# An encoder layer's attention leaves its softmax undivided until the output projection loads it, and VectorE takes a further share of the modulation's half columns

## The chip, the cores and the metric

The kernel runs on one core of one Trainium2 chip. That core has TensorE (PE in the profile; its weight loads are PEld), VectorE (DVE), ScalarE (ACT), GpSimd (POOL) and SyncE (SP), which here issues nearly all of the DMA transfers. The metric is the device time of one execution in microseconds (us); lower is better.

## What is computed

The layer takes x (1024 positions of 1024 features) and a conditioning vector c, and returns x after a mixer and a feed-forward part, in float32. The parts that the change touches are these:

```python
cond = jax.nn.silu(c)
mod = cond @ w_ada[l] + b_ada[l]                       # w_ada is 1024 x 6144
sh1, sc1, g1, sh2, sc2, g2 = jnp.split(mod, 6, axis=-1)
h = modulate(rms_norm(x, norm_mix_g[l]), sh1, sc1)
proj = h @ w_in[l]                                     # q, k, v of attention; qk, v, o, gates of the mLSTM
q_a, k_a, v_a, qk_m, v_m, o_m, gates = jnp.split(proj, splits, axis=-1)
y_attn = axial_gqa_attention(q_a, k_a, v_a, ...)       # 8 heads of 64, 2 heads of keys and values
y_mem = bidirectional_mlstm(qk_m, v_m, o_m, gates, ...)
mix = jnp.concatenate([y_attn, y_mem], axis=-1) @ w_out[l]
x = x + g1[:, None, :] * mix
...
# in axial_gqa_attention, for each block of 128 queries:
    s = jnp.einsum('bkgqd,bksd->bkgqs', q_blk, kt).astype(jnp.float32) * scale
    p = jax.nn.softmax(s, axis=-1).astype(vt.dtype)    # exp(s - max) / sum
    return jnp.einsum('bkgqs,bksd->bkgqd', p, vt)
```

The division by the sum is a factor for each query and head. It can be put on p (1024 numbers for each query) or on the product of p with the values (64 numbers for each query and head).

## The kernel before

**Precision.** A product of the projections is made of three matmuls (`mm3`, L322 to L325): both operands are split into a high and a low part (names ending in hi/lo or h/l), and high by high, low by high and high by low are summed in PSUM. ScalarE makes the high part as a copy, VectorE or GpSimd the low part as a subtraction. Each tile that is loaded for a projection so needs ScalarE and then VectorE or GpSimd before TensorE can use it.

**Stages** (times of the profiled execution): modulation and the first projections to about 142 us, the entry to attention to 161, attention to 485, the entry to the mLSTM to about 500, the mLSTM with the output projection to about 660, then the feed-forward part and the end at 1326.

**What sets the order of the work.** One Python program writes all engines' instructions in one order, and each engine executes its own in that order. The order is found by a planner inside the kernel: `Clock` keeps an estimated time for each engine (`Engine.cost`), `ck.chain` appends steps each of which is emitted once the one before is estimated to be done, and `streams` emits TensorE's work from several generators, the mains first and the fills where no main is ready. An entry of `bg` makes a step wait in the plan until its engine is free. So a step with another estimated cost can move all instructions that come after it. Nearly every operation of VectorE, ScalarE and GpSimd is emitted in one helper and has line L102; groups are told apart by tiles. DMAs have L328, and SyncE issues them in the written order: one that must wait holds those behind it.

**Modulation.** `w_ada` is read in columns of 128. The 64 half columns from column 16 on are loaded by `ada_late`, two ahead (`bufs=ahead`). While the list `calm` is not empty (until attention begins), VectorE multiplies a half with `cond` and sums it in one instruction (9 halves, tiles `ada<-ada,cond` on DVE). Later GpSimd multiplies and ScalarE sums as it copies (55 halves: `ada<-ada,cond` on POOL and `ada<-ada` on ACT).

**Attention** goes over 64 blocks q, 8 heads of 8 blocks each. `scores` issues four matmuls of 128x512 into S (L1202), and chains: VectorE takes the maximum (`sst<-S`) and scales it, ScalarE makes P = exp(...) with the sum of each row into the small tile `sst`, VectorE takes the reciprocal of the sum, GpSimd multiplies P by it in place (`norm`, L1217, `P<-P,sst`). Only then is the flag `Pok` set, on which `turned` waits: 8 transposes of 128x128 on TensorE (T, L1234), a copy PT of the high part on ScalarE, and the low part on VectorE. `values` multiplies with the values (`av`, L1255), ScalarE and VectorE bring the result to `avt`, and a DMA writes it to the DRAM tiles `ya_d`. There are three tiles P and 8 tiles sst. The fills between are the units of the list `IN` (the rest of the input projection; "acc" for the column-wise units q and f, followed by normalisation or by the convolution's steps `xp` and `y`, and "acct" for the units t, which ScalarE copies to `vstg`).

**The entry to attention.** `att_q(0)` makes the tile `qs` of the first head: a copy on ScalarE, then a subtraction on VectorE. Ahead of it the gates of the mLSTM are prepared; the steps `soft` (ScalarE) and `logf` (VectorE, `T<-T,gt`) end with the flag `logf_ok`, and the tile `qs` lies where `gt` was. A later step, `moved`, copies T to `Fr` on ScalarE.

**The mLSTM and the output projection** run together: transposes and products of the mLSTM (`tr<-mq,mk` L2015, U L1962, with `wv` of GpSimd and `mq` loaded by SyncE), and as fills the units of `MIX`, which are rows of the output projection. `load_y` loads the projection's input: for attention (`mem` false) the tiles `yat` from `ya_d`, 4 for each half n of the positions; `yah` and `yal` are their high part (ScalarE) and low part (GpSimd). Also the last units of IN (acct) end in this stage.

Of the kernel before, what the change touches and what calls it, by code (L numbers as in the profile page):

```python
# [20 lines left out]
P = 128  # L21
# [25 lines left out]
AHEAD = 2  # L47
NP = NF // 2
IN = [("q", 2), ("q", 3), ("f", 0), ("f", 4), ("t", 2), ("f", 1),
      ("f", 5), ("f", 2), ("t", 1), ("f", 6), ("f", 3), ("f", 7), ("t", 3)]  # L50
MIX = [("o", i) for i in range(16)] + [("m", (i + 8) % 16) for i in range(16)]
FF = [("b", p) for p in range(NB)] + [("v", 0)] + [("s", (p, i)) for p in range(1, NP - 1) for i in range(2)] + [("v", NP - 1)]
SET = ["A11", "A12", "S2", "S3", "S1", "A22", "S4"]
# [207 lines left out]
def layer_kernel(ctx, tc, xT, c, w_ada, vecs, cons, rope, w_f, w_fT, w_t0, w_t, w_o, w_gu, w_d, out):  # L261
# [39 lines left out]
    mqk_d = [dram.tile([P, S], F32, name=f"mqk_d{i}") for i in range(8)]  # L301
    v_d = [dram.tile([P, NJ, 2, P], F32, name=f"v_d{i}") for i in range(2)]
    o_d = [dram.tile([P, NJ, 2, P], F32, name=f"o_d{i}") for i in range(2)]
    ya_d = [dram.tile([P, S], F32, name=f"ya_d{i}") for i in range(4)]
    x1_d = [dram.tile([P, S], F32, name=f"x1_d{i}") for i in range(KT)]
    act_d = [{m: dram.tile([P, HALF], F32, name=f"act_d{p}{m}") for m in DOWN} for p in range(NP)]
# [20 lines left out]
    def dma(dst, src, q=None):  # L327
        (q or nc.sync).dma_start(dst, src)  # L328
        on_chip = dst.space == src.space == bass.MemoryType.SB if hasattr(src, "space") else False
        return ck.dma(math.prod(dst.shape) * 4, 0.65 if on_chip else 0.5)  # L330
# [45 lines left out]
    with tc.manual_schedule():  # L376
# [777 lines left out]
        def ada_late(ahead=2):  # L1154

            n = len(adas)
            if n == 64 or n >= ahead and not (adas[n - ahead].done and adas[n - ahead].t <= ck.t):
                return
            j, i = 16 + n // 2, n % 2
            t = PP["ada"].tile([P, HALF], F32, tag="ada", name="ada", bufs=ahead)  # L1160
            if calm:
                adas.append(ck.chain(dma(t, w_ada[j][:, halves(i)]), lambda: dve.scalar_tensor_tensor(
                    t, t, 1.0, PP["cond"][:, halves(i)], op0=OP.mult, op1=OP.mult, accum_out=modacc[:, i, j:j + 1]),
                    bg=["dve"]))
                return
            adas.append(ck.chain(dma(t, w_ada[j][:, halves(i)]), lambda: gps.tensor_mul(t, t, PP["cond"][:, halves(i)]),
                                 lambda: act.activation(t, t, AF.Copy, accum_out=modacc[:, i, j:j + 1]),
                                 bg=["gps", "act"]))
# [9 lines left out]
        def att_q(h):  # L1178
            if h:
                qd = ap.tile([P, S], F32, tag="qd", name="qd", bufs=1)  # L1180
                src = q_d[h // 2][(h % 2) * DH:(h % 2 + 1) * DH]
                dma(qd[0:DH], src)
                there = ck.chain(dma(qd[DH:P], src), lambda: None)
            else:
                qd, there = q0_at
            qs = ap.tile([P, S], F32R, tag="qs", name="qs")
            Q[h] = qs, ck.chain(0.0, there, lambda: act.activation(qs, qd, AF.Copy),
                                lambda: (gps if h else dve).tensor_sub(qs[DH:P], qd[DH:P], qs[DH:P].bitcast(F32)))

        def scores():  # L1190

            for q in range(NQ):
                h, j = divmod(q, NJ)
                if j == 2 and h + 1 < AH:
                    att_q(h + 1)
                ada_late()
                g, (qs, ok) = h // 4, Q[h]
                yield [ok, k2_ok[g]] + [slot("S")] + Tem[max(q - 3, 0):max(q - 2, 0)]
                sp, f = psum_tile([P, S], "S")
                for n in range(NH):  # L1200
                    for m in range(2):
                        nc.tensor.matmul(sp[:, halves(n)], qs[:, j * P:(j + 1) * P], k2[g][m][:, halves(n)],  # L1202
                                         start=m == 0, stop=m == 1)
                ck.pe(0.87)
                st = ap.tile([P, 4], F32, tag="sst", name="sst", bufs=8)
                cq = colq[:, j, h:h + 1]

                def top(st=st, sp=sp, cq=cq):
                    dve.reduce_max(st[:, 0:1], sp, axis=AX.X)
                    dve.tensor_scalar(st[:, 1:2], st[:, 0:1], cq, -1.0, op0=OP.mult, op1=OP.mult)  # L1210

                def exp(st=st, sp=sp, cq=cq, q=q, f=f):
                    Pt[q] = ap.tile([P, S], F32, tag="P", name="P", bufs=3)
                    act.activation(Pt[q], sp, AF.Exp, bias=st[:, 1:2], scale=cq, accum_out=st[:, 2:3])
                    f.set(ck, ck.fin + LAT)

                def norm(st=st, q=q):  # L1217
                    gps.tensor_scalar(Pt[q], Pt[q], st[:, 3:4], 0.0, op0=OP.mult, op1=OP.add)

                ck.chain(LAT, top, exp, lambda st=st: dve.reciprocal(st[:, 3:4], st[:, 2:3]), norm, flag=Pok[q])  # L1220

        def turned():

# [50 lines left out]
        def load_y(mem, n):  # L1274
# [6 lines left out]
            for k in range(4):  # L1281
# [5 lines left out]

                def load(e=e, k=k):
                    t = op.tile([P, HALF], F32, tag="yat", name="yat", bufs=4)
                    arrive = dma(t, (ym_d if mem else ya_d)[k][:, halves(n)])  # L1290

                    def hi():
# [4 lines left out]
                        e[1] = op.tile([P, HALF], F32R, tag="yal", name="yal", bufs=yb)  # L1297
                        gps.tensor_sub(e[1], t, e[0].bitcast(F32))

                    ck.chain(arrive, *used, hi, lo, flag=e[2])  # L1300

                ck.chain((2.0 if mem else 0.0) + (2.5 * k if at else 0.0), *([ym_ok[k][n]] if mem else []), load)

# [1089 lines left out]
```

## Time and profile before

Three runs took 1324.91, 1325.05 and 1332.57 us; the median is 1325.05. The profiled execution took 1328.24 us, of which the span from the first to the last instruction is 1326.4, at a mean granted TensorE clock of 0.991.

| stage of the profiled execution | us | PE busy | DVE busy | ACT busy | POOL busy | granted clock |
|---|---|---|---|---|---|---|
| entry to attention, 142 to 161 | 19 | 11.02 | 18.11 | 7.24 | 6.40 | 0.82 |
| attention, 161 to 485 | 324 | 303.18 | 266.10 | 238.31 | 205.53 | 1.00 |
| in the mLSTM, 500 to 580 | 80 | 77.13 | 66.64 | 49.56 | 41.80 | 1.00 |
| whole span | 1326.4 | 1268.8 | 1044.1 | 705.8 | 524.5 | 0.991 |

In the rows of groups, "out<-in" names the tiles, then come their sizes, the count, the total busy time, the mean of one in ns, and after the second bar the engine's idle time just before, with the work that ended most of it. In rows of the timeline the first two numbers are start and length in us; a bracket at the end holds the idle time before and what ended it. In rows of waits come the total in us, how often, and the longest.

### The profile page before, as it was taken

To read this page: it belongs to the slowest core of one execution; us is meant where nothing else is said; L and a number is where in the kernel's file an instruction comes from. 1 tells how busy PE (TensorE), PEld (TensorE's weight loads), DVE (VectorE), ACT (ScalarE), POOL (GpSimd) and SP (SyncE) were. 2 spreads that over 40 slices of the span, in tenths; PEclk is the share of its full clock that TensorE was granted. 3 is DMA by queue.
4 is the path that set the end of the run, shared out by engine and by line. 5 is a ranking of instruction groups with operands and counts; after the bars stand their busy time and mean duration, and the time that the engine had idled before them with its cause. 6 is when DMAs were issued, how large, how long until landed. Compare 5 with 4: busy or idle time off the path is not lost.

```text
span 1326.4 us, 19735 instructions
## 1 busy us (share of the span) xinstructions
PE 1268.8 (96%) x6656; PEld 1071.9 (81%) x6656; DVE 1044.1 (79%) x1679; ACT 705.8 (53%) x1349; POOL 524.5 (40%) x455
## 2 busy tenths in 40 slices
PE   9999789999899999999999999999999998999997
PEld 7887678878887888787877888888888886888886
DVE  7958798879578956898789988866676755788886
ACT  6583667877587746555686332233332334454453
POOL 0072467766476515532153355544555420000002
PEclk9999899999999999999999999999999999999999
DMA  9547423333233237633552443323333259733324
GB/s 375 196 151 196 127 99 121 96 94 106 81 120 94 64 117 259 202 100 124 191 184 71 159 135 128 112 104 115 109 104 110 88 192 335 274 100 93 94 60 163
DMA packets 104469, 187.04 MB, mean 141 GB/s; under 512 B 11568, under 2 KB 33200, under 8 KB 104368
## 3 DMA queue, kind: packets, MB, share of 16 engines
q1 hardware_dynamic: 91120, 163.81, 38.1%
q10 hardware_dynamic: 13248, 21.97, 4.4%
q8 instruction: 53, 0.87, 0.3%
q14 instruction: 48, 0.39, 0.1%
HBM read 139.33 MB, written 42.73 MB: 137 GB/s over the span
## 4 chain that ended last, share of the span: by engine, by line
PE 65%; DVE 16%; ACT 6%; DMA 5%; issue 4%; POOL 4%; SPq 0%; ACTq 0%; DVEq 0%; POOLq 0%
PE acc L325 16%; PE acc L323 16%; PE acc L324 16%; DVE x L102 3%; PE av L1255 3%; PE T L1234 3%; PE S L1202 2%; DVE sst L102 2%; DVE y L102 2%; DVE PT L102 2%; DVE wlo L102 1%; PE acct L323 1%; POOL wlo L102 1%; PE acct L325 1%; PE acct L324 1%
## 5 line engine op out<-in xcount | busy, mean ns | idle before, releaser
L102 ACT ACTIVATE whi<-wst 128x512 fp32r<-128x512 f32 (+2 forms) x223 | 133.9, 607 | 140.8 <-PE acc L325 62.7
L102 POOL TENSOR_TENSOR wlo<-wst,whi 128x512 fp32r<-128x512 f32 x80 | 123.2, 1547 | 162.3 <-ACT whi L102 110.9
L324 PE MATMUL acc<-x,whi 128*128 128x512 f32 x352 | 136.9, 389 | 0.0
L102 DVE TENSOR_TENSOR wlo<-wst,whi 128x512 fp32r<-128x512 f32 (+2 forms) x143 | 94.3, 664 | 33.2 <-ACT whi L102 32.8
L102 POOL TENSOR_SCALAR P<-P,sst 128x1024 f32<-128x1024 f32 x64 | 84.3, 1319 | 77.3 <-DVE sst L102 69.0
L102 DVE TENSOR_TENSOR PT<-T,PT 128x512 fp32r<-128x512 f32 x128 | 84.8, 682 | 24.7 <-ACT PT L102 24.4
L323 PE MATMUL acc<-hh,whi 128*128 128x512 f32 x224 | 96.2, 429 | 8.4 <-ACT xp L102 8.4
L102 POOL TENSOR_TENSOR x<-x,ny 128x256 f32<-128x256 f32 (+1 forms) x8 | 8.3, 1066 | 237.3 <-PE acc L325 217.1
L102 POOL TENSOR_TENSOR wlo<-wr,whi 128x512 fp32r<-128x512 f32 x52 | 72.2, 1388 | 71.8 <-ACT whi L102 68.7
L325 PE MATMUL acc<-whi,wcl 128*128 128x512 f32 x244 | 96.6, 396 | 2.6 <-DVE wcl L102 2.6
L323 PE MATMUL acc<-whi,wch 128*128 128x512 f32 x244 | 96.2, 394 | 2.3 <-ACT wch L102 2.3
L324 PE MATMUL acc<-wlo,wch 128*128 128x512 f32 x244 | 95.9, 393 | 0.0
L324 PE MATMUL acc<-hl,whi 128*128 128x512 f32 x224 | 88.7, 396 | 0.3 <-DVE hl L102 0.3
L102 ACT ACTIVATE whi<-wr 128x512 fp32r<-128x512 f32 x56 | 35.4, 632 | 100.6 <-DVE wr L102 48.3
L102 POOL TENSOR_TENSOR ada<-ada,cond 128x512 f32<-128x512 f32 x55 | 78.6, 1435 | 25.7 <-DMA ada<-in_w_ada_dram 22.6
L325 PE MATMUL acc<-hh,wlo 128*128 128x512 f32 x224 | 88.7, 396 | 0.1
L102 ACT ACTIVATE P<-S,sst,colq 128x1024 f32<-128x1024 f32 x64 | 77.2, 1206 | 21.1 <-DVE sst L102 20.7
L102 ACT ACTIVATE PT<-T 128x512 fp32r<-128x512 f32 x128 | 73.5, 597 | 26.7 <-PE T L1234 25.4
L323 PE MATMUL acct<-whi,hh 128*128 128x256 f32 (+1 forms) x256 | 77.6, 303 | 9.5 <-ACT vstg L102 8.8
L102 DVE TENSOR_REDUCE sst<-S 128x1 f32<-128x1024 f32 x64 | 77.7, 1214 | 6.2 <-PE S L1202 5.1
L1234 PE MATMUL T<-ident,P 128*128 128x128 f32 x512 | 72.8, 274 | 6.6 <-DVE PT L102 4.0
L324 PEld LDWEIGHTS acc<-x,whi 128*128 128x128 f32 x352 | 66.1, 188 | 13.7
(483 smaller groups left out, 3836.6 us busy)
## 6 DMA issues: line engine op xcount, KB each, us to landing
wr<-in_w_gu_dram SPq DMA_DIRECT2D x66, 256.0 KB, 2.7
ada<-in_w_ada_dram SPq DMA_DIRECT2D x64, 256.0 KB, 2.9
wd<-in_w_d_dram SPq DMA_DIRECT2D x22, 512.0 KB, 6.9
wst<-in_w_gu_dram SPq DMA_DIRECT2D x42, 256.0 KB, 2.9
wst<-act_d SPq DMA_DIRECT2D x33, 256.0 KB, 3.1
ada<-in_w_ada_dram SPq DMA_DIRECT2D x16, 512.0 KB, 7.4
wst<-in_w_o_dram SPq DMA_DIRECT2D x32, 256.0 KB, 3.3
act_d<-sg ACTq DMA_DIRECT2D x29, 256.0 KB, 2.1
```

Of the source, the lines that this page charges most:

```text
L102: return fn(*args, **kw)
L323: nc.tensor.matmul(acc, w[0], x[0], start=first, stop=False)
L324: nc.tensor.matmul(acc, w[0], x[1], start=False, stop=False)
L325: nc.tensor.matmul(acc, w[1], x[0], start=False, stop=last)
L1202: nc.tensor.matmul(sp[:, halves(n)], qs[:, j * P:(j + 1) * P], k2[g][m][:, halves(n)], start=m == 0, stop=m == 1)
L1234: nc.tensor.transpose(tp[:, k], Pt[q][:, (4 * b + k) * P:(4 * b + k + 1) * P], ident)
L1255: nc.tensor.matmul(av, va[:, k, h // 4], PT[it, b][m][:, k - 4 * b], start=(k, m) == (0, 0), stop=(k, m) == (NJ - 1, 1))
```

## The change

The reciprocal of the sums and its multiplication with P go away from the 64 blocks. exp now puts its sums into `colq`, the tile whose column (the scale of this block's scores) it has just used. When the last block of a head has its P, VectorE takes the reciprocal of that head's 8 columns in one instruction, and a DMA writes the 1024 numbers to a new DRAM tile `r_d`. `load_y` reads them for attention's halves: before each `yat`, two DMAs spread the numbers of two heads over 64 partitions each of a tile `yar` (two such tiles), and GpSimd multiplies `yat` by `yar` before `yah` and `yal` are made.

Beside this, `ada_late` gives every second half column to VectorE also during attention, where the planner's estimate has VectorE free within 0.3 us: 12 halves move, so that VectorE has 21 and GpSimd and ScalarE 43. The first head's `qs` is chained behind `logf_ok`, and in `IN` the unit f 6 comes before t 1.

```diff
--- before.py
+++ after.py
@@ -47,7 +47,7 @@
 AHEAD = 2
 NP = NF // 2
 IN = [("q", 2), ("q", 3), ("f", 0), ("f", 4), ("t", 2), ("f", 1),
-      ("f", 5), ("f", 2), ("t", 1), ("f", 6), ("f", 3), ("f", 7), ("t", 3)]
+      ("f", 5), ("f", 2), ("f", 6), ("t", 1), ("f", 3), ("f", 7), ("t", 3)]
 MIX = [("o", i) for i in range(16)] + [("m", (i + 8) % 16) for i in range(16)]
 FF = [("b", p) for p in range(NB)] + [("v", 0)] + [("s", (p, i)) for p in range(1, NP - 1) for i in range(2)] + [("v", NP - 1)]
 SET = ["A11", "A12", "S2", "S3", "S1", "A22", "S4"]
@@ -301,6 +301,7 @@
     mqk_d = [dram.tile([P, S], F32, name=f"mqk_d{i}") for i in range(8)]
     v_d = [dram.tile([P, NJ, 2, P], F32, name=f"v_d{i}") for i in range(2)]
     o_d = [dram.tile([P, NJ, 2, P], F32, name=f"o_d{i}") for i in range(2)]
+    r_d = [dram.tile([1, S], F32, name=f"r_d{i}") for i in range(AH)]
     ya_d = [dram.tile([P, S], F32, name=f"ya_d{i}") for i in range(4)]
     x1_d = [dram.tile([P, S], F32, name=f"x1_d{i}") for i in range(KT)]
     act_d = [{m: dram.tile([P, HALF], F32, name=f"act_d{p}{m}") for m in DOWN} for p in range(NP)]
@@ -1158,7 +1159,7 @@
                 return
             j, i = 16 + n // 2, n % 2
             t = PP["ada"].tile([P, HALF], F32, tag="ada", name="ada", bufs=ahead)
-            if calm:
+            if calm or ck.free["dve"] <= ck.now + 0.3 and n % 2:
                 adas.append(ck.chain(dma(t, w_ada[j][:, halves(i)]), lambda: dve.scalar_tensor_tensor(
                     t, t, 1.0, PP["cond"][:, halves(i)], op0=OP.mult, op1=OP.mult, accum_out=modacc[:, i, j:j + 1]),
                     bg=["dve"]))
@@ -1184,7 +1185,7 @@
             else:
                 qd, there = q0_at
             qs = ap.tile([P, S], F32R, tag="qs", name="qs")
-            Q[h] = qs, ck.chain(0.0, there, lambda: act.activation(qs, qd, AF.Copy),
+            Q[h] = qs, ck.chain(0.0, there, *([] if h else [logf_ok]), lambda: act.activation(qs, qd, AF.Copy),
                                 lambda: (gps if h else dve).tensor_sub(qs[DH:P], qd[DH:P], qs[DH:P].bitcast(F32)))
 
         def scores():
@@ -1211,13 +1212,14 @@
 
                 def exp(st=st, sp=sp, cq=cq, q=q, f=f):
                     Pt[q] = ap.tile([P, S], F32, tag="P", name="P", bufs=3)
-                    act.activation(Pt[q], sp, AF.Exp, bias=st[:, 1:2], scale=cq, accum_out=st[:, 2:3])
+                    act.activation(Pt[q], sp, AF.Exp, bias=st[:, 1:2], scale=cq, accum_out=cq)
                     f.set(ck, ck.fin + LAT)
 
-                def norm(st=st, q=q):
-                    gps.tensor_scalar(Pt[q], Pt[q], st[:, 3:4], 0.0, op0=OP.mult, op1=OP.add)
-
-                ck.chain(LAT, top, exp, lambda st=st: dve.reciprocal(st[:, 3:4], st[:, 2:3]), norm, flag=Pok[q])
+                ck.chain(LAT, top, exp, flag=Pok[q])
+                if j == NJ - 1:
+                    rq = colq[:, :, h]
+                    ck.chain(1.0, *Pok[q - j:q + 1], lambda rq=rq: dve.reciprocal(rq, rq),
+                             lambda rq=rq, h=h: dma(r_d[h].rearrange("o (j p) -> p (o j)", p=P), rq), bg=[None] * NJ + ["dve", None])
 
         def turned():
 
@@ -1287,6 +1289,9 @@
 
                 def load(e=e, k=k):
                     t = op.tile([P, HALF], F32, tag="yat", name="yat", bufs=4)
+                    r = None if mem else op.tile([P, HALF], F32, tag="yar", name="yar", bufs=2)
+                    for i in range(0 if mem else 2):
+                        dma(r[i * DH:(i + 1) * DH], r_d[2 * k + i][:, halves(n)].partition_broadcast(DH))
                     arrive = dma(t, (ym_d if mem else ya_d)[k][:, halves(n)])
 
                     def hi():
@@ -1297,7 +1302,7 @@
                         e[1] = op.tile([P, HALF], F32R, tag="yal", name="yal", bufs=yb)
                         gps.tensor_sub(e[1], t, e[0].bitcast(F32))
 
-                    ck.chain(arrive, *used, hi, lo, flag=e[2])
+                    ck.chain(arrive, *used, *([] if mem else [lambda: gps.tensor_mul(t, t, r)]), hi, lo, flag=e[2])
 
                 ck.chain((2.0 if mem else 0.0) + (2.5 * k if at else 0.0), *([ym_ok[k][n]] if mem else []), load)
 
```

TensorE has the same instructions as before (6422 rows of the program), in another order.

**ScalarE at the entry to attention**, before. Tiles have running numbers; `xp` is the convolution's or the projection's input step, `whi` a weight's high part, `P` the first block's exp.

```order
L102 ACTIVATE xp_1411<-acc_1482 128x512 [waits PE_49]
L102 ACTIVATE qs_1584<-qd0_1337 128x1024 [waits DMAHW0_49,DVE_49,Pool_49]
L102 ACTIVATE xp_1529<-acc_1532 128x512 [waits PE_49]
L102 ACTIVATE Fr_1601<-T1_1373 64x1024
L102 ACTIVATE whi_1607<-wst_1508 128x512 [waits DMAHW7_49,PE_49]
L102 ACTIVATE ada_1585,modacc_81<-ada_1585 128x512 [waits Pool_49]
L102 ACT_TABLE_LOAD [waits DVE_49,PE_49]
L102 ACTIVATE P_1646,sst_1620<-S_1612,sst_1620,colq_190 128x1024 [waits Activation_49]
```

And after:

```order
L102 ACTIVATE xp_1419<-acc_1490 128x512 [waits PE_49]
L102 ACTIVATE Fr_1596<-T1_1381 64x1024 [waits DVE_49]
L102 ACTIVATE qs_1592<-qd0_1345 128x1024 [waits DMAHW0_49,Pool_49]
L102 ACTIVATE xp_1537<-acc_1540 128x512 [waits PE_49]
L102 ACTIVATE whi_1615<-wst_1516 128x512 [waits DMAHW7_49,PE_49]
L102 ACT_TABLE_LOAD [waits DVE_49]
L102 ACTIVATE xp_1419<-y_1558 128x1024 [waits Activation_49]
L102 ACTIVATE whi_1656<-wst_1560 128x512 [waits DMAHW1_49,PE_49]
L102 ACTIVATE xp_1537<-acc_1595 128x512 [waits PE_49,Activation_49]
L102 ACTIVATE P_1659,colq_198<-S_1629,sst_1634,colq_198 128x1024 [waits DVE_49]
```

`Fr`, the copy behind the gates, now stands ahead of `qs` and of the second `xp`, on which the next matmuls wait. The half column (`ada` with `modacc`) is no longer ahead of the first P, two steps of the convolution are.

**SyncE at the first loads of the output projection**, before. `o_d` is a store of the input projection's last units, `mq` a load for the mLSTM; DMAHW names stand for earlier transfers that a DMA waits for.

```order
L328 DMA o_d1_100<-vstg_5540 128x256 [waits Activation_49]
L328 DMA yat_5570<-ya_d0_101 128x512
L328 DMA yat_5572<-ya_d1_102 128x512
L328 DMA yat_5574<-ya_d2_103 128x512 [waits DMAHW0_49]
L328 DMA yat_5576<-ya_d3_104 128x512 [waits DMAHW1_49]
L328 DMA o_d1_100<-vstg_5568 128x256 [waits DMAHW2_49,Activation_49]
L328 DMA mq_5602<-mqk_d0_89 128x256 [waits DMAHW3_49]
```

And after, from the first `yat` on (its two `yar` stand just ahead of these rows):

```order
L329 DMA yat_5454<-ya_d0_109 128x512 [waits DMAHW0_49]
L329 DMA yar_5460<-r_d2_103 64x512 [waits DMAHW1_49]
L329 DMA yar_5460<-r_d3_104 64x512 [waits DMAHW2_49]
L329 DMA yat_5459<-ya_d1_110 128x512 [waits DMAHW3_49]
L329 DMA yar_5465<-r_d4_105 64x512 [waits DMAHW6_49,DMAHW7_49,DMAHW4_49,Pool_49]
L329 DMA yar_5465<-r_d5_106 64x512 [waits DMAHW5_49]
L329 DMA yat_5464<-ya_d2_111 128x512
L329 DMA yar_5470<-r_d6_107 64x512 [waits DMAHW2_49,DMAHW1_49,Pool_49]
L329 DMA yar_5470<-r_d7_108 64x512 [waits DMAHW0_49]
L329 DMA yat_5469<-ya_d3_112 128x512
L329 DMA o_d1_100<-vstg_5452 128x256 [waits Activation_49]
L329 DMA mq_5498<-mqk_d0_89 128x256 [waits DMAHW3_49]
```

Each `yat` now has two `yar` ahead of it. The third and fourth pair wait for GpSimd, which must have used the first and second tile, and the load of `mq` stands behind all twelve transfers and a store.

**GpSimd at the same place**, before. `wv` are the mLSTM's weighted values, four for each step, the first of which waits for TensorE.

```order
L102 TENSOR_SCALAR wv_5590<-v1_5498,cols_191 128x130 [waits DMAHW1_49,Pool_49]
L102 TENSOR_SCALAR wv_5590<-v1_5498,cols_191 128x130 x3
L102 TENSOR_SCALAR wv_5651<-v1_5498,cols_191 128x130 x4
L102 TENSOR_TENSOR yal_5664<-yat_5570,yah_5648 128x512 [waits DMAHW6_49,Activation_49]
L102 TENSOR_TENSOR yal_5679<-yat_5572,yah_5662 128x512 [waits DMAHW7_49,Activation_49]
L102 TENSOR_SCALAR wv_5682<-v1_5498,cols_191 128x130 [waits PE_49]
L102 TENSOR_SCALAR wv_5682<-v1_5498,cols_191 128x130 x3
L102 TENSOR_TENSOR yal_5694<-yat_5574,yah_5674 128x512 [waits DMAHW0_49,Activation_49]
L102 TENSOR_TENSOR yal_5706<-yat_5576,yah_5690 128x512 [waits DMAHW1_49,Activation_49]
L102 TENSOR_SCALAR wv_5709<-v1_5498,cols_191 128x130 [waits PE_49]
```

And after:

```order
L102 TENSOR_SCALAR wv_5545<-v1_5382,cols_199 128x130 x4
L102 TENSOR_TENSOR yat_5454<-yat_5454,yar_5455 128x512 [waits DMAHW7_49,DMAHW6_49,DMAHW0_49]
L102 TENSOR_SCALAR wv_5563<-v1_5382,cols_199 128x130 [waits PE_49]
L102 TENSOR_SCALAR wv_5563<-v1_5382,cols_199 128x130 x3
L102 TENSOR_TENSOR yat_5459<-yat_5459,yar_5460 128x512 [waits DMAHW3_49,DMAHW2_49,DMAHW1_49]
L102 TENSOR_TENSOR yal_5598<-yat_5454,yah_5585 128x512 [waits Activation_49]
L102 TENSOR_TENSOR yat_5464<-yat_5464,yar_5465 128x512 [waits DMAHW6_49,DMAHW5_49,DMAHW4_49]
L102 TENSOR_SCALAR wv_5590<-v1_5382,cols_199 128x130 [waits PE_49]
L102 TENSOR_SCALAR wv_5590<-v1_5382,cols_199 128x130 x3
L102 TENSOR_TENSOR yat_5469<-yat_5469,yar_5470 128x512 [waits DMAHW7_49,DMAHW1_49,DMAHW0_49]
L102 TENSOR_TENSOR yal_5637<-yat_5459,yah_5625 128x512 [waits Activation_49]
L102 TENSOR_TENSOR yal_5677<-yat_5464,yah_5664 128x512 [waits Activation_49]
```

The new multiplications of `yat` by `yar` stand in turn with `wv`: one group of `wv` is between the first and the second of them, another between the third and the fourth.

## The prediction

> **What bounds the kernel now.** I read the page's first part, then the stretches in which the change lies.
>
> ```profile
> PE 1268.8 (96%) x6656; PEld 1071.9 (81%) x6656; DVE 1044.1 (79%) x1679; ACT 705.8 (53%) x1349; POOL 524.5 (40%) x455
> ```
>
> TensorE is busy for 96% of the span and keeps its instructions, so nothing can be won but its idle time and its slow clock. The stretches' columns are start and end, length, busy time of PE, PEld, DVE, ACT and POOL, granted clock, DMA share, GB/s:
>
> ```profile
> 142.00:161.00 19.00, 11.02 (x38) 8.25 (x37) 18.11 (x22) 7.24 (x11) 6.40 (x4) 0.82 0.43 138
> 161.00:485.00 324.00, 303.18 (x2014) 269.02 (x2014) 266.10 (x420) 238.31 (x479) 205.53 (x159) 1.00 0.30 94
> ```
>
> In attention TensorE idles 20.8 of 324 us, beside 8 us at the entry, where the clock also drops. No other engine is full there. What TensorE waits for from 140 to 500 us (total, times, longest):
>
> ```profile
> PE acct L323 <- ACT vstg L102: 8.8, 9, 2.0
> PE acc L323 <- ACT xp L102: 8.4, 3, 4.8
> PE T L1234 <- DVE PT L102: 4.0, 6, 1.6
> PE S L1202 <- ACT P L102: 3.2, 1, 3.2
> PE T L1234 <- POOL P L102: 2.0, 3, 1.6
> PE av L1255 <- DVE PT L102: 1.4, 3, 0.7
> ```
>
> The last steps are copies and subtractions that free or fill a buffer. Only 2.0 us are put down to GpSimd's division directly. The change must work through what stands ahead of these steps in their engines' queues.
>
> **The attention part.** The removed and moved work, per group:
>
> ```profile
> L102 POOL TENSOR_SCALAR P<-P,sst 128x1024 f32<-128x1024 f32 x64 | 84.3, 1319 | 77.3 <-DVE sst L102 69.0 <-PE T L1234 4.0 <-ACT PT L102 3.2
> L102 POOL TENSOR_TENSOR ada<-ada,cond 128x512 f32<-128x512 f32 x55 | 78.6, 1435 | 25.7 <-DMA ada<-in_w_ada_dram 22.6 <-ACT PT L102 3.0
> ...
> L102 DVE SCALAR_TENSOR_TENSOR y<-xp,vec,y 128x1024 f32<-128x1024 f32 x32 | 48.6, 1520 | 0.3
> ...
> L102 ACT ACTIVATE ada<-ada 128x512 f32<-128x512 f32 x55 | 34.6, 631 | 19.6 <-POOL ada L102 19.6
> ...
> L102 DVE RECIPROCAL sst<-sst 128x1 f32<-128x1 f32 x64 | 10.0, 157 | 16.6 <-ACT P L102 16.2
> ```
>
> ```profile
> L102 DVE SCALAR_TENSOR_TENSOR ada<-ada,cond 128x512 f32<-128x512 f32 x9 | 8.1, 907 | 8.2 <-DMA ada<-in_w_ada_dram 8.2
> ```
>
> Engine by engine: GpSimd loses 84.3 us of division and 12 x 1.435 = 17.2 of halves, half of its 205.5. ScalarE loses 12 x 0.631 = 7.6. VectorE loses 10.0 and gains 12 x 0.907 = 10.9 and eight wider reciprocals, at least 8 x 0.157 = 1.3: 2 us more. So VectorE, the fullest engine beside TensorE, gets no relief. None of these sums is on the path; what counts is whom they hold up. Two such places:
>
> ```profile
> 421.94 2.02 POOL L102 TENSOR_SCALAR P<-P,sst 128x1024 f32<-128x1024 f32 x1 [1.89 <-DVE sst L102]
> 423.92 2.23 POOL L102 TENSOR_TENSOR ada<-ada,cond 128x512 f32<-128x512 f32 x1
> ```
>
> ```profile
> 426.19 0.63 ACT L102 ACTIVATE ada<-ada 128x512 f32<-128x512 f32 x1 [2.12 <-POOL ada L102]
> ```
>
> ```profile
> 427.45 0.50 PE L323 MATMUL acc<-hh,whi 128*128 128x512 f32 x1 [2.91 <-ACT xp L102]
> ```
>
> ```profile
> 174.21 0.39 PE L323 MATMUL acct<-whi,hh 128*128 128x256 f32 x1 [2.00 <-ACT vstg L102]
> ```
>
> At 424 GpSimd's half stands behind a division, ScalarE waits 2.12 us for it, its next step `xp` comes late, and TensorE stands 2.91 us. At 174 it is the same, with `vstg`. Without divisions GpSimd takes each half as it lands, so I take both stalls as gone: -4.9 us (bounds -4.9 and 0). The direct wait for P goes too, -2.0 (bounds -2.0 and 0). Of the waits for PT, 5.4 us, I take -1.0: T now starts some 1.5 us sooner after exp, but VectorE's queue is no shorter and its order is new (bounds -4 and +3, the one near the sum of both rows, the other near what two new rows like them would cost). The other `vstg` waits have no cause here that goes: 0 (-3 to +5).
>
> A rule that speaks against the moved halves: the Trainium skill, "SBUF — State Buffer", section "Who interferes with whom", says that a VectorE instruction with two SBUF inputs and a GpSimd instruction that reads SBUF exclude one another for their whole length. The trace agrees in kind: a step y beside which GpSimd did nothing took
>
> ```profile
> 158.90 1.28 DVE L102 SCALAR_TENSOR_TENSOR y<-xp,vec,y 128x1024 f32<-128x1024 f32 x1
> ```
>
> against a mean of 1.52 in attention. By this row VectorE gains up to 32 x 0.24 = 7.7 us of time when the divisions go; I put it at no gain on the path, and it is a reason for the first rival.
>
> **The entry to attention.** ScalarE now, contiguous to the dots:
>
> ```profile
> 146.13 1.06 ACT L102 ACTIVATE qs<-qd 128x1024 fp32r<-128x1024 f32 x1 [3.70 <-issue]
> 147.09 0.58 ACT L102 ACTIVATE xp<-acc 128x512 f32<-128x512 f32 x1
> 147.69 1.06 ACT L102 ACTIVATE Fr<-T 64x1024 f32<-64x1024 f32 x1
> ...
> 157.39 0.63 ACT L102 ACTIVATE ada<-ada 128x512 f32<-128x512 f32 x1 [3.94 <-POOL ada L102]
> ```
>
> `qs` stood until 146.13, and `xp` behind it ended TensorE's wait of 4.8 us. The chaining to `logf_ok` doesn't remove this, since the tile waited for that step anyway; and `Fr`, 1.06 long, now stands ahead of both: +1.1. Ahead of the first P stood the half column, itself 3.94 us late; it is away from there, so of the 3.2 us that S waited for P I take 2.6 as gone (two other steps stand ahead of P now). Together -1.5 (bounds -3.2 and +2).
>
> **The entry to the mLSTM.** SyncE, the landings (count, size, us) and those who wait:
>
> ```profile
> 495.04 2.20 SPq L328 DMA_DIRECT2D yat<-ya_d  x4
> 497.35 0.37 SPq L328 DMA_DIRECT2D o_d<-vstg  x1
> 498.62 0.32 SPq L328 DMA_DIRECT2D mq<-mqk_d  x1
> ```
>
> ```profile
> mq<-mqk_d SPq DMA_DIRECT2D x16, 128.0 KB, 3.1
> yat<-ya_d SPq DMA_DIRECT2D x8, 256.0 KB, 5.9
> ```
>
> ```profile
> 505.30 0.61 PE L2015 MATMUL tr<-mq,mk 128*128 128x128 f32 x4
> 505.66 0.36 PE L323 MATMUL acct<-whi,hh 128*128 128x256 f32 x1
> 505.86 0.28 PE L324 MATMUL acct<-wlo,hh 128*128 128x256 f32 x1
> 505.98 0.28 PE L325 MATMUL acct<-whi,hl 128*128 128x256 f32 x1
> ```
>
> ```profile
> 504.47 1.44 POOL L102 TENSOR_SCALAR wv<-v,cols 128x130 f32<-128x130 f32 x4
> ```
>
> ```profile
> L102 POOL TENSOR_TENSOR yal<-yat,yah 128x512 fp32r<-128x512 f32 x14 | 18.9, 1355 | 32.3 <-ACT yah L102 29.4 <-DMA yat<-ya_d 2.8
> ```
>
> `mq` was issued at 498.62 and used at 505.30, with 3.6 us to spare after its 3.1. Now SyncE issues, at 0.55 us each (2.20 for four), two `yar` and the first `yat` (issued at 496.1, landed after 5.9 at 502.0), the second three, and then stands until GpSimd has multiplied the first `yat` (1.36, priced as `yal`: 503.4). Behind that GpSimd has four `wv` (1.44: 504.8) and the second product (506.2), on which SyncE's fourth triple waits. Three issues and a store make it 508.4 for `mq`, which lands at 511.5. By the order of the instructions, TensorE has 18 more acct matmuls ahead of its use, 0.12 us apart, so it comes at 505.30 + 2.2 = 507.5: a stall of 4.0 us. The second half's four loads have the same shape later; nothing in the trace shows how near it is to its use, so it lies between 0 and another 4.0, and I take 1.0, as those loads are planned further ahead. Together +5.0 (0 to +9).
>
> The eight writes of `r_d`, 1024 numbers of 4 bytes each, have no like row; DMA is busy 0.30 of the stretch, and the last is due some 20 us after attention ends: 0, at worst a later fourth triple.
>
> **The sum.** -4.9 - 2.0 - 1.0 - 1.5 + 5.0 = -4.4 us. The profiled execution would take 1328.24 - 4.4 = 1323.8; it lies 3.2 above the median, so on the median of 1325.05 the forecast is 1320.6. The terms' distances to their ends, squared and added, give roots of 6.8 downwards and 9.8 upwards: its own range is 1314 to 1330. Chance 0.50.
>
> **The rivals.**
>
> *All queue waits go.* With GpSimd half empty and its claim on VectorE's inputs gone, PT comes early too, and `mq` is absorbed: 4.9 + 2.0 + 5.4 + 3.2, half of the remaining vstg waits (3.4), less 1.1 for `Fr` is 17.8: 1307. For it speaks the mean of 1.52 for y; against it that VectorE stays at 266 of 324 us. Chance 0.20.
>
> *Slower: SyncE stands behind GpSimd.* If `mq` behind the added transfers lands as late as `yat` (5.9), it is there at 514.3 and TensorE stands 6.8 us, and the second half costs 4 more. At 142 to 161 an idle of 4.8 us came with a clock of 0.82, worth up to 0.18 x 19 = 3.4 us, where the stall of 2.91 at 427 left it at 1.00; I add 2.4. With an attention gain of 5 that is +8: 1333. It decides once `mq` lands after about 512.5. For it speaks that every step was summed without slack; against it that TensorE still has matmuls of the output projection that a planner may put there. Chance 0.18. The Trainium skill, "TensorE: Matmul & The Clock Gate", section "What's actually happening", puts the limit at an idle window of about 3.4 us and halves the clock for as long again; the two rows agree. By it the forecast's own stall of 4.0 would also cost some 1.7 us, which is inside its range.
>
> *Nothing to see.* The new order makes as many waits for `vstg` and PT as it removes (the +5 above), and the gain and loss cancel: 1325. Chance 0.12.
>
> **Range and chances.** 1305 to 1333 takes in all centres and leaves out the far ends of the first two rivals. A measurement here can tell about 1% from no change (1311.8 to 1338.3). Faster than that: nearly all of the first rival, 0.19. Slower: a third of the second, 0.06. Within: 0.75.
>
> **What would show it.** Right: no wait of ScalarE for GpSimd's `ada` above 1 us in attention, T waiting for ScalarE's P not at all, the first `xp` wait grown to about 5.9, `tr<-mq,mk` waiting 3 to 5 us for `mq` near 508, GpSimd's busy time in attention near 105 us. Wrong: waits for PT or `vstg` beyond 20 us together, or a clock below 1.00 after 500 us.

## The result and the profile after

The changed kernel takes 1398.63 us (median of 4 runs, 1397.23 to 1401.17) where the kernel before, beside it, takes 1326.28: a ratio of 1.0533, 95% interval 1.0511 to 1.0555. The forecast was 1320.6 with a range up to 1333. It was wrong by 78 us and in the direction.

The page of the changed kernel, its first line and, by the same columns as before, three stretches: the entry, attention, and ten microseconds in attention.

```profile
PE 1286.0 (92%) x6656; PEld 1089.6 (78%) x6656; DVE 1048.4 (75%) x1647; ACT 698.2 (50%) x1325; POOL 431.8 (31%) x387
```

```profile
142.00:165.00 23.00, 13.78 (x50) 10.69 (x49) 21.08 (x27) 11.05 (x17) 6.87 (x5) 0.76 0.34 104
165.00:550.00 385.00, 318.55 (x2004) 284.30 (x2002) 264.30 (x390) 229.54 (x454) 106.50 (x83) 0.91 0.34 80
199.00:209.00 10.00, 6.02 (x43) 5.29 (x41) 3.47 (x6) 3.22 (x7) 0.00 (x0) 0.98 0.27 27
```

GpSimd's load in attention fell as forecast, from 205.5 to 106.5 us. TensorE's busy time rose by 17 us over the whole span with the same number of matmuls; the granted clock in attention is 0.91 where it was 1.00, and TensorE idles 66 us there instead of 21. In the third row TensorE stands for 4 of the 10 us, VectorE and ScalarE for more than 6, GpSimd for all of them, and the transfers move 27 GB/s at a busy share of 0.27. In attention before the change they moved 94 GB/s at 0.30.

Who waits, by the first rows of waits of the changed kernel (TensorE's alone from 167 to 560 us, then three rows of all engines from 161 to 535):

```profile
PE T L1236 <- DVE PT L102: 28.7, 6, 11.2
PE av L1257 <- ACT PT L102: 16.4, 2, 8.3
PE acct L324 <- ACT vstg L102: 9.7, 5, 7.3
PE acc L324 <- ACT xp L102: 7.0, 3, 4.9
```

```profile
POOL ada L102 <- DMA ada<-in_w_ada_dram: 117.1, 20, 14.2
...
ACT qs L102 <- DMA qd<-q_d: 29.8, 3, 12.1
...
ACT ada L102 <- POOL ada L102: 21.0, 4, 9.8
```

The waits for PT and `vstg` are over 50 us together, which is the first of the prediction's own signs of being wrong (more than 20). These are few and long waits, not many short ones: ScalarE stands six times, once after each of the first six stores, for 6.6 to 12.1 us behind a transfer that came late. The first of them from its beginning, one row each of SyncE, GpSimd, ScalarE and TensorE:

```profile
195.26 0.40 SPq L329 DMA_DIRECT2D r_d<-colq  x1
195.76 1.42 SPq L329 DMA_DIRECT2D ada<-in_w_ada_dram  x1
```

```profile
210.75 1.26 POOL L102 TENSOR_TENSOR ada<-ada,cond 128x512 f32<-128x512 f32 x1 [12.96 <-DMA ada<-in_w_ada_dram]
```

```profile
212.05 0.63 ACT L102 ACTIVATE ada<-ada 128x512 f32<-128x512 f32 x1 [9.78 <-POOL ada L102]
```

```profile
213.30 1.95 PE L1257 MATMUL av<-PT,va 128*128 128x256 f32 x5 [8.29 <-ACT PT L102]
```

SyncE issues the store of the first head's reciprocals, then a half column, which lands 14.9 us later. GpSimd so starts on it only at 210.75, ScalarE its product at 212.05, the copy PT comes behind that, and TensorE stands 8.29 us and then finds its clock at 0.50 (209 to 215 us). What the store itself takes from issue to landing, in the list of DMA issues (count, size, median us):

```profile
r_d<-colq SPq DMA_DIRECT2D x8, 4.0 KB, 13.5
```

A store of 4 KB needs 13.5 us (one of the eight landings is recorded in this trace), where 256 KB of a half column need 2.9 in the median. From 195 to 199 us 1078 of the 1344 packets on record are under 512 bytes; from 199 to 209 us it is 14 of 153. The store's 1024 pieces are so on record within 4 us of its issue, but it lands at 208.8, and the other transfers are slow until then. What passes in these ten us the packets don't tell.

Stage by stage, in us, by the starts of the first S, the first and the second block of `tr<-mq`, the last `tr<-mq`, and the down projection's first product with `wch`; the last column is an experiment below, in which only the store's pieces are larger:

| stretch | before | after | stores of 32-byte pieces |
|---|---|---|---|
| start to first S | 153.6 | 159.1 | 157.4 |
| first S to first tr | 343.7 | 403.3 | 337.1 |
| first to second block of tr | 8.0 | 15.5 | 15.5 |
| to the last tr | 98.6 | 98.0 | 98.0 |
| to the down projection | 502.0 | 504.2 | 505.3 |
| to the end | 220.4 | 217.1 | 217.4 |

Of the 71 us between the spans, 60 come in attention.

### The profile page after: what moved, and what is told of

It reads as the page before. It is cut to its first block, busy times and chain, and to the rows that moved or that the text cites. A ratio compares the mean times of both kernels' runs of the same rounds, so it can differ in the third digit from the quotient of the medians.

```text
span 1397.2 us, 19494 instructions
## 1 busy us (share of the span) xinstructions
PE 1286.0 (92%) x6656; PEld 1089.6 (78%) x6656; DVE 1048.4 (75%) x1647; ACT 698.2 (50%) x1325; POOL 431.8 (31%) x387
## 4 chain that ended last, share of the span: by engine, by line
PE 61%; DVE 16%; DMA 11%; ACT 4%; issue 4%; POOL 3%; SPq 1%; ACTq 0%; DVEq 0%; POOLq 0%
PE acc L326 16%; PE acc L324 15%; PE acc L325 15%; PE T L1236 3%; PE av L1257 3%; DVE x L102 3%; DMA ada<-in_w_ada_dram 2%; PE S L1203 2%; DMA qd<-q_d 2%; DVE PT L102 2%; DVE y L102 1%; DVE sst L102 1%; PE acct L324 1%; PE acct L326 1%; PE acct L325 1%
## 5 line engine op out<-in xcount | busy, mean ns | idle before, releaser
L1236 PE MATMUL T<-ident,P 128*128 128x128 f32 x512 | 78.3, 290 | 29.4 <-DVE PT L102 28.7
L102 POOL TENSOR_TENSOR ada<-ada,cond 128x512 f32<-128x512 f32 x43 | 62.0, 1446 | 126.5 <-DMA ada<-in_w_ada_dram 117.1
L1257 PE MATMUL av<-PT,va 128*128 128x256 f32 x512 | 76.0, 294 | 20.6 <-ACT PT L102 16.4
L1236 PEld LDWEIGHTS T<-ident,P 128*128 128x128 f32 x512 | 64.0, 149 | 37.1 <-DVE PT L102 30.7
L324 PE MATMUL acct<-whi,hh 128*128 128x256 f32 (+1 forms) x256 | 80.8, 316 | 11.8 <-ACT vstg L102 9.7
L1257 PEld LDWEIGHTS av<-PT,va 128*128 128x128 f32 x512 | 69.0, 196 | 25.9 <-ACT PT L102 17.0
```

Of the source, the lines that this page charges most:

```text
L102: return fn(*args, **kw)
L324: nc.tensor.matmul(acc, w[0], x[0], start=first, stop=False)
L1236: nc.tensor.transpose(tp[:, k], Pt[q][:, (4 * b + k) * P:(4 * b + k + 1) * P], ident)
L1257: nc.tensor.matmul(av, va[:, k, h // 4], PT[it, b][m][:, k - 4 * b], start=(k, m) == (0, 0), stop=(k, m) == (NJ - 1, 1))
```

## The experiments

Theory A: a store of 1024 single numbers holds up the transfers behind it. Theory B: the new order and the moved half columns cost the time.

**The stores alone.** Edit on the kernel before:

```diff
...
                 ck.chain(LAT, top, exp, lambda st=st: dve.reciprocal(st[:, 3:4], st[:, 2:3]), norm, flag=Pok[q])
+                if j == NJ - 1:
+                    rq = colq[:, :, h]
+                    ck.chain(1.0, *Pok[q - j:q + 1], lambda rq=rq, h=h: dma(r_d[h].rearrange("o (j p) -> p (o j)", p=P), rq))
```

> The kernel before, with nothing of the change but the eight stores to r_d, at the same places (they store the scale columns of colq, and nobody reads them; the output is that of the kernel before). Theory A, that a store of 1024 single numbers holds up the transfers queued behind it: the changed kernel lost 10 to 14 us in most heads after its stores, so 1326 plus 50 to 75, that is 1376 to 1401, with the stall of ScalarE or GpSimd on a late load of queries or halves once per head. Theory B, that the new order and the moved half columns cost the time: within 1% of 1326.

Measured: ratio 1.0199 (1.0166 to 1.0232), 28 us on the spans (1354.0 against 1326.4). Eight stores of 4 KB that nobody reads cost 2%. The landings of this kernel:

```profile
r_d<-colq SPq DMA_DIRECT2D x8, 4.0 KB, 10.4
```

Six of them are recorded, at 9.6 to 11.7 us. Theory A's mechanism is there, but with 28 us where 50 to 75 were expected.

**Larger pieces.** Edit on the changed kernel; the partition's 8 numbers are put side by side on both sides:

```diff
-                    ck.chain(1.0, *Pok[q - j:q + 1], lambda rq=rq: dve.reciprocal(rq, rq),
-                             lambda rq=rq, h=h: dma(r_d[h].rearrange("o (j p) -> p (o j)", p=P), rq), bg=[None] * NJ + ["dve", None])
+                    rc = ap.tile([P, NJ], F32, tag="rc", name="rc", bufs=2)
+                    ck.chain(1.0, *Pok[q - j:q + 1], lambda rq=rq, rc=rc: dve.reciprocal(rc, rq),
+                             lambda rc=rc, h=h: dma(r_d[h].rearrange("o (p j) -> p (o j)", p=P), rc), bg=[None] * NJ + ["dve", None])
```

> The changed kernel, with the reciprocals put into a small contiguous tile and stored as 128 runs of 8 numbers (32 bytes) instead of 1024 single numbers; the loads then read the numbers in another order, so the attention half of the output projection's input is divided by the wrong sums. All instructions otherwise in the same order. Theory A: most of the 72 us goes, 1320 to 1340. Theory B: stays at 1390 to 1400.

Measured: ratio 1.0009 (0.9991 to 1.0026), span 1330.5. All of the loss but 4 us on the span is gone, with everything else of the change in place: in the two traces every engine has the same instructions in the same order, and only the store's pieces differ. (This kernel divides by the wrong sums; that changes numbers, not work.) The store of this kernel:

```profile
r_d<-rc SPq DMA_DIRECT2D x8, 4.0 KB, 1.7
```

And who waits on late transfers in attention (all engines, 161 to 510 us):

```profile
POOL ada L102 <- DMA ada<-in_w_ada_dram: 95.0, 26, 8.9
...
ACT qs L102 <- DMA qd<-q_d: 1.9, 2, 1.3
...
ACT ada L102 <- POOL ada L102: 1.5, 2, 1.2
```

ScalarE hardly stands for queries or halves any more (1.3 us at most). Theory B falls as the main cause. GpSimd still waits 95 us for halves, but nobody waits long for it, so this is idle time that it has.

**Single numbers at other places.** Edit on the changed kernel:

```diff
-dma(r_d[h].rearrange("o (j p) -> p (o j)", p=P), rq)
+dma(r_d[h].rearrange("o (p j) -> p (o j)", p=P), rq)
```

> The changed kernel, where only the places in DRAM change: still 1024 single numbers of 4 bytes, but the 8 numbers of a partition lie side by side in r_d (read in another order by the loads, so divided by the wrong sums). Theory A by the number of pieces: as slow as the changed kernel, 1390 to 1400. Theory A by scattered addresses in DRAM: near the kernel with runs of 32 bytes. Theory B: 1390 to 1400 too; this one tells the two forms of A apart.

Measured: ratio 1.0289 (1.0207 to 1.0371), span 1359.9, landings of 7.1 to 11.6 us:

```profile
r_d<-colq SPq DMA_DIRECT2D x8, 4.0 KB, 8.3
```

Between the two forms. About half of the loss goes when a partition's numbers lie together in DRAM, and the rest stays as long as they are 1024 pieces: both count. How much each counts is rough, since the two runs of this kernel lie 15 us apart (1361.71 and 1376.76), and the trace is of the faster one.

**The stores on another queue.** Edit: the store gets `nc.scalar` as its issuing engine.

> The changed kernel with the eight stores of single numbers issued by ScalarE instead of SyncE, so that they stand in another DMA queue; TensorE's instructions are the same. If the stores only hold up what stands behind them in their own queue, nearly all of the 72 us goes: 1330 to 1345, with the numbers landing as late as before. If they occupy the DMA engines themselves, or the way to DRAM, the transfers of the other queue are held up as well: 1380 to 1400.

Measured: ratio 1.0320 (1.0290 to 1.0351), span 1367.2. It lies between both statements. All transfers from 244 to 251 us, behind the second store, which ScalarE issued at 242.84, and the store `ya_d` that SyncE issued at 244.89 (64 KB, landing after 9.2 us; 1.9 is the median of this store in the changed kernel):

```profile
DMA packets 888, 0.12 MB, mean 17 GB/s; under 512 B 805, under 2 KB 869, under 8 KB 887
```

```profile
ya_d<-avt SPq DMA_DIRECT2D x1, 64.0 KB, 9.2
```

SyncE's transfers still trickle though the store stands in another queue, so what is held is shared by the queues. Some 30 us come back; how much of that is the queue, and how much that ScalarE now issues the stores, the run doesn't tell. The Trainium skill, "DMA: Bandwidth & Descriptors", section "Issuing engines are not separate DMA queues", says that transfers run on the same 16 DMA engines whoever starts them; the 17 GB/s agree with it.

**Why 28 us become 70.** Two more kernels complete a square of division (on GpSimd as before, or left to the loads) and halves (moved or not), all with the stores of single numbers. The changed kernel with `if calm:` as before:

> The changed kernel with its stores of single numbers, but all half columns after the start of attention with GpSimd and ScalarE, as before (55 and 9). The stores alone cost 28 us in the kernel before and 68 in the changed one. If the moved halves make the difference (VectorE's queue standing for a half that lands late): 1355 to 1370. If the removed division does (GpSimd and ScalarE now reach each half at once and stand there when it lands late): 1390 to 1400.

And the kernel before with the stores and the new condition:

> The kernel before (division on GpSimd kept, its load_y kept) with the eight stores of single numbers and the rule that gives VectorE every second half column (13 move). The fourth corner beside three that are known on the time: stores with division and no halves moved +28 us over before, stores without division and no halves moved +52, stores without division and halves moved +72. If the moved halves cost the same with the division as without it (20): 1373 to 1381. If GpSimd's division is what covers a late transfer, whoever takes the halves: 1352 to 1364.

Measured: ratios of 1.0394 (1.0367 to 1.0421) and 1.0217 (1.0184 to 1.0250). Spans, less the 1326.4 of before:

| | halves not moved | halves moved |
|---|---|---|
| division on GpSimd | +28 | +31 |
| division at the loads | +52 | +71 |

With the division, the moved halves cost 3 us on the span, which the ratios don't tell from nothing (1.0199 and 1.0217, with intervals that overlap); without it, 19. The lower row has the rest of the change too: the loads of `yar`, the chained first queries and the new order of units. Rows of waits of the kernel with division and without moved halves, and then of the one without either (all engines, 161 to 510):

```profile
POOL ada L102 <- DMA ada<-in_w_ada_dram: 31.2, 14, 6.1
...
ACT ada L102 <- POOL ada L102: 19.5, 16, 2.3
...
ACT qs L102 <- DMA qd<-q_d: 12.5, 4, 8.4
```

```profile
POOL ada L102 <- DMA ada<-in_w_ada_dram: 108.6, 24, 16.7
...
ACT ada L102 <- POOL ada L102: 24.2, 8, 7.6
...
ACT qs L102 <- DMA qd<-q_d: 17.0, 3, 9.3
```

With the division in its queue, GpSimd comes to a half late anyway, and one that lands 10 us late keeps ScalarE no longer than 2.3 us. Without it ScalarE stands up to 7.6 us behind GpSimd's halves (9.8 in the changed kernel). By the plan that is because each step of a half then follows right on the landing that the planner expects; no run shows this step by itself. Waits of TensorE above 3.3 us between the first S and the last av are 2, 3, 6 and 6 in the order stores alone, with halves, without division, changed kernel; they sum to 11, 18, 41 and 48 us, and at each the granted clock falls to 0.50 for 3.4 us or more. That division was cover for late halves fits all of this, and the kernel with division and moved halves came out as that account had it; but it isn't shown by itself, because each of these kernels has its own planned order and the lower row more changes than the division. Why the moved halves cost 19 without the division stays open.

**Turned on TensorE.** The repair that computes the same as the changed kernel: a head's 128x8 reciprocals are transposed into PSUM, and the store has 8 rows of 512 bytes.

```diff
-                             lambda rq=rq, h=h: dma(r_d[h].rearrange("o (j p) -> p (o j)", p=P), rq), bg=[None] * NJ + ["dve", None])
+                    def turn(rq=rq, h=h):
+                        rp, f = psum_tile([P, 4, P], "T")
+                        nc.tensor.transpose(rp[0:NJ, 0], rq, ident)
+                        ck.add_pe(0.06)
+                        rt = ap.tile([DH, 2, P], F32, tag="avt", name="rt", bufs=3)[0:NJ, 0]
...
+                        ck.chain(0.3, take, lambda: dma(r_d[h].rearrange("o (j p) -> (o j) p", p=P), rt))
...
```

> The changed kernel, with each head's 128x8 reciprocals transposed by TensorE into PSUM and copied by ScalarE to 8 rows of 128, so that the store has 8 runs of 512 bytes. 8 more small matmuls and 8 small copies. Theory A: 1318 to 1335, the forecast of before with its other terms put to the test. Theory B: above 1385.

Measured: ratio 1.0048 (1.0025 to 1.0071), span 1330.7; the median of 1336.55 lies 4 us above the profiled execution. Without the moved halves:

> The version with the numbers transposed by TensorE (8 runs of 512 bytes), without the moved halves. The forecast's term: the moved halves bring nothing of themselves, so the same within 4 us as the version with them (1331 on the trace). Rival, the port between VectorE and GpSimd: 12 fewer VectorE instructions of 0.9 us and no gain for GpSimd, 5 to 8 us faster. Rival, ScalarE's waits for GpSimd's halves come back: 5 us slower.

Measured: 1.0059 (1.0041 to 1.0077), span 1332.3, so the moved halves are worth nothing that can be seen once the stores are cheap, as the forecast had it; neither rival shows.

**Four tiles yar.** Edit on the version turned on TensorE: `bufs=4` in place of `bufs=2`.

> The version with the numbers transposed by TensorE, with four tiles yar instead of two: the same order of transfers, but the third and fourth triple no longer wait for GpSimd, so SyncE reaches the load of mq some 4 to 8 us sooner. If that wait made TensorE's stall of 4.4 us for mq: the stall is below 1 us and the span 3 to 5 us shorter, 1326 to 1328. If the bytes of the eight added loads ahead of mq made it: the stall stays at 3 to 5 us.

Measured: 1.0016 (1.0001 to 1.0031), span 1330.9. TensorE's first matmul on `mq` of the second block, with two tiles and then with four:

```profile
507.89 0.98 PE L2032 MATMUL tr<-mq,mk 128*128 128x128 f32 x3 [4.37 <-DMA mq<-mqk_d]
```

```profile
507.03 0.68 PE L2032 MATMUL tr<-mq,mk 128*128 128x128 f32 x4 [1.70 <-DMA mq<-mqk_d]
```

The stall falls by 2.7 us, so SyncE's wait for GpSimd made most of it. It doesn't fall below 1 us, as expected; the added issues and bytes may make the remaining 1.7, which no run shows. The span doesn't follow: the entry to attention was longer by about as much in this run (first S at 157.8 against 155.8). On the ratios it is 0.3% better, with intervals that overlap.

**Three attempts at the rest.** All start from the version with four tiles. The first head's queries without the chain behind the gates:

> The version turned by TensorE with four tiles yar, with the first head's queries no longer chained behind the gates: on ScalarE qs stands ahead of Fr again and the half column's place is unchanged. The forecast's price of Fr at that place is 1.1 us; the versions with the chain show TensorE's first wait for xp at 5.8 to 7.4 us, the kernel before 4.8. If Fr's place is the cause: the wait falls to 4.5 to 5.2 and the span by 1 to 3 us, 1328 to 1330, on the time at par with before or up to 0.2% faster. If something else holds qs: the wait stays at about 6.4.

Measured: 1.0078 (1.0059 to 1.0096). `Fr` stood behind `qs` again and the wait was 6.5 us all the same. That looks as if its place cost nothing, but the step of VectorE on which `Fr` and `qs` wait (`logf`, `T<-T,gt`) came later here. Starts on VectorE and of the `xp` behind `qs`, in us:

| kernel | `T<-T,gt` | `xp` | between |
|---|---|---|---|
| before | 143.88 | 147.09 | 3.21 |
| 32-byte pieces, chained | 145.04 | 149.29 | 4.25 |
| four tiles, chained | 145.54 | 149.78 | 4.24 |
| four tiles, not chained | 146.66 | 149.88 | 3.22 |

So `Fr` ahead of `qs` costs 1.0 us, as the forecast had it, and without the chain a start 1.1 us later hides it. The trace is of the slowest of the six runs (1344.51, median 1339.60). Its span, 1342.6, was lost later, in attention (346.3 us from first S to first tr, against 336.6) and in the mLSTM, where a wait of 4.0 us for VectorE's `num` went with a clock of 0.50. The units in the old order:

> The version turned by TensorE with four tiles yar, with the two units f 6 and t 1 in the order of before; the chain stays. Nothing in the forecast gave the swap a price of its own: the same within 3 us as the version with it (span 1330.9). Rival: the swap was what kept the convolution ahead of the mLSTM's loads, and without it the entry to the mLSTM is 3 to 8 us later.

Measured: 1.0061 (1.0038 to 1.0084), span 1333.2. The spans differ by 2.3 us, but the ratios by 0.45%, 6 us, with intervals that don't meet (1.0001 to 1.0031 with the swap); and the first `tr<-mq` starts at 498.4 where it was 494.4, within the rival's 3 to 8 us. So the expectation of no difference fails: the swap, which the forecast gave no price, seems to be worth some us. That the convolution is the reason isn't shown. The loads of `yar` issued by ScalarE, without the chain:

> As the one whose first queries aren't chained, with the sixteen loads yar issued by ScalarE. SyncE has only the yat ahead of mq, so if its issues (0.55 us each) make what is left of the stall for mq (1.7 us), the stall goes and the span falls by 1.5 to 3 us. If ScalarE stands at its own issues (they wait for store and slots), the copies behind it come late: 2 to 10 us slower.

Measured: 1.0122 (1.0095 to 1.0148), span 1338.8 in the fastest of four runs: the wait for `mq` is gone, but ScalarE stands 11.0 us at its own issues and TensorE 5.4 us for the `vstg` behind them. Against the version without the chain the time is some 6 us longer, by the ratios, as expected for that case. No version was faster than the kernel before.

## Why the prediction was wrong

**The step that failed** is the eight writes of `r_d`, put at "0, at worst a later fourth triple". They cost 67 us of the 71 on the spans: between the changed kernel and the one with pieces of 32 bytes nothing else differs in the order of the instructions. Two arguments behind that 0 were bad. The DMA's busy share of 0.30 was taken as room; but at 199 to 209 us the share is 0.27 while transfers that are due come 10 us late, so a low share doesn't tell room. And only the last store was asked when it is needed, not what stands behind each in the queue: halves, queries and weights. That the operation had "no like row" should have widened the range upwards, by at least eight times some unknown hold, and didn't.

The Trainium skill, "DMA: Bandwidth & Descriptors", section "Rules for kernel authors", says that a last dimension that isn't contiguous is lowered to one descriptor for each element and should be rearranged. Such a store is this one, and that was a rival to weigh. The trace agrees with the count: more than 1024 packets under 512 bytes within 4 us of the issue. The rule gives no price; the runs do: 9.6 to 13.5 us for 1024 pieces in the changed kernel and with the stores alone, 1.7 in the median for 128.

**The other terms**, read from the kernel with 32-byte pieces. Its rows of TensorE's waits, 140 to 520 us:

```profile
PE acc L324 <- ACT xp L102: 8.8, 3, 6.7
PE tr L2021 <- DMA mq<-mqk_d: 5.7, 2, 4.6
PE T L1237 <- DVE PT L102: 5.5, 6, 2.2
PE av L1258 <- DVE PT L102: 4.0, 5, 1.6
PE acct L324 <- ACT vstg L102: 2.9, 5, 1.0
PE acct L324 <- ACT xp L102: 2.4, 2, 2.2
```

- ScalarE's waits for GpSimd's halves: forecast to go (-4.9). They fell from 19.6 us (the entry included) to 1.5. Right. TensorE's waits for `vstg` fell from 8.8 to 2.9, of which only 2.0 was forecast; the other `vstg` waits, put at 0 (-3 to +5), so gave -3.9.
- T waiting for P from GpSimd (-2.0): gone. Right.
- Waits for PT (-1.0, bounds -4 and +3): 9.5 in place of 5.4, so +4.1. Wrong in sign, just beyond the upper bound.
- The entry (-1.5): the wait for `xp` is 6.7 where 5.9 was forecast, and in place of S's wait for P (3.2) there is one of acct for `xp` (2.2). First S comes 3.8 us later, of which six more matmuls ahead of it, 0.23 us apart, are 1.4. So +2.4 before first S, where the sum had only `Fr` (+1.1). The price of `Fr` was right, 1.0 us by the table above; what the sum left out is that VectorE's `T<-T,gt` starts 1.2 us later (145.04 against 143.88), because ScalarE's steps on the gates, behind the copies of `k`, already start 1.2 us later (133.98 against 132.79).
- The entry to the mLSTM (+5.0): the stall for `mq` is 4.61, forecast 4.0. SyncE stood from 495.97 to 501.60 before the third triple, as the forecast had it, and 18 more acct matmuls stand ahead of the use. Right, and by the named mechanism. The 1.0 for the second half isn't seen as a wait for `mq`.

```profile
495.64 0.33 SPq L329 DMA_DIRECT2D yat<-ya_d  x1
501.60 1.08 SPq L329 DMA_DIRECT2D yar<-r_d  x2
502.73 0.59 SPq L329 DMA_DIRECT2D yat<-ya_d  x1
```

From first S to first tr that kernel is 6.6 us shorter, of which the six acc matmuls that moved ahead of first S are 1.4: a gain of 5.2. The forecast for this stretch was 7.9 for attention and 2.6 for S's wait, 10.5 together. So without the failed step the change would have been the third rival, nothing to see: ratio 1.0009 (0.9991 to 1.0026), where the sum of the other terms, -4.4 us, would be 0.9967. The rest of the sum was some 6 us too hopeful by the ratios (8.5 by the spans), mostly in attention, by the waits for PT above all.

**The port.** The prediction allowed VectorE up to 7.7 us from the end of the divisions, if these lengthened the steps y beyond 1.28 us. Their mean was 1520 ns with divisions; in the kernel with 32-byte pieces, without them:

```profile
L102 DVE SCALAR_TENSOR_TENSOR y<-xp,vec,y 128x1024 f32<-128x1024 f32 x32 | 50.2, 1570 | 0.5
```

No gain: taking the divisions away did not shorten them.

**The slower rival** had a wrong place (SyncE behind GpSimd at the mLSTM, which cost 4.6 us and not 6.8) and a right second half: each wait above 3.3 us came with a granted clock of 0.50, and of the 60 us lost in attention about 15 are the longer busy time of TensorE at a clock of 0.91 (318.55 against 303.18).

## What to carry to other kernels

Before a store is priced, count the contiguous pieces that it falls into on each side, not its bytes: here 4 KB in 1024 pieces slowed all transfers of the core for some 10 us, and in 128 pieces cost nothing that could be seen. For a DMA that is added, look at what is issued in the 15 us behind it and who waits for that, since the DMA's busy share stays low while they are late (0.27 here). And work that is taken off an engine that isn't the bound may have been cover for late transfers: ask who stands there when the engine arrives on time. When two versions are compared by one trace each, look where these traces lie among the runs: here some were the fastest and some the slowest.

## What had not been expected of the hardware

A small store slowed not only its own queue but the other engine's as well (17 GB/s in all at 244 to 251 us with the store on ScalarE's queue). Its packets were on record within 4 us, ten before it landed. Where the numbers lie in DRAM matters beside their count (a ratio of 1.0289 against 1.0533 for the same 1024 pieces; the landings, 7.1 to 11.6 us against 9.6 to 13.5, overlap). And the same 4 KB stores cost 28 us in one order of work and some 70 in another.
